# State-space input matrices built with (position, channel) on the partitions from factor rows in DRAM, and the kernel's own data moved to GpSimd's DMA queue

## The chip, the cores and the metric

One Trainium2 chip, one core. The metric is the device time of the whole program in microseconds. Before the change it is 1427.78 us, the median of three runs (1423.44 to 1439.42).

## The reference, cut to what matters

Two layers of a hybrid encoder over 256 positions of width 1024. Each layer has three branches (retention, latent attention, and a state-space layer, S5), gates, an output projection and a SwiGLU feed-forward network. The change touches the S5 branch alone in what it computes. S5 has 64 groups of 16 channels; each drives 64 complex states, in two directions d:

```python
mag = jnp.exp(dt * ar)
abar_re, abar_im = mag * jnp.cos(dt * a_im), mag * jnp.sin(dt * a_im)
bb_re = coef_re[..., None] * b_re - coef_im[..., None] * b_im
bb_im = coef_re[..., None] * b_im + coef_im[..., None] * b_re
bu = einsum('bsgc,gpc->bsgp', u_g, bb)      # complex
x_t = abar * x_{t-1} + bu_t                 # scan over s, forward for d=0, backward for d=1
y = Re(C x)                                 # summed over both directions
```

## The kernel before

**What dominates.** Nearly all weights are multiplied in three passes: ScalarE casts a raw weight tile of 512 KB to a high part (`wh`, L668), VectorE takes the rest (`wl`, L669), and TensorE runs three matmuls for each 128 rows of it (L673 to L675). A weight tile is thus 24 matmuls of 256 columns. Raw tiles come through SP's DMA queue into five buffers. This is the foreground.

**S5 is a background.** `s5` is a generator. `tick` gives it credit each time the foreground has emitted a tile or two, and a step of it is emitted while there is credit. The framework then orders the instructions of each engine by its own forecast; each engine runs its list in that order. Layer 0's S5 begins with the program; layer 1's begins before the feed-forward network of layer 0 (`begin(l + 1)`), so that its tables and matrices are made beside that network.

**Blocks of eight positions.** The scan runs over 32 blocks of 8 positions. For each of 16 steps `qq` (4 groups of channels each) an input matrix WT is needed that takes 8 positions x 16 channels = 128 rows to 256 columns (2 directions x re/im x 64 states). It is the product of a power of abar (by position) with bb (by channel). `s5_wt` makes it with the states on the partitions: VectorE multiplies a table of powers (`PW`) by `BB` in three products of 512 columns (L523, L526 twice) and adds the shared one to the other two (L531, 1024 columns). TensorE then turns it in 8 transposes of 128x128 (L536) through two PSUM banks of the pool `p5`, and ScalarE copies each bank out (L538). TensorE multiplies it with the input U in 4 matmuls (L452). After every second step ScalarE copies the product out (L459), TensorE transposes it (L462), and ScalarE writes it to the states SS in 8 small copies (L467, L468). Of `p5`'s two banks one holds the product over two steps.

Layer 0 makes WT when it is used. Layer 1 makes all 16 early, writes them to DRAM (`wtd`) and reads them back when its U is there.

**Tables.** `s5_params` makes the powers `pn` and the coefficients `cf` with (direction, group) on the partitions. `s5_tables` turns them by matmuls with a permutation (L299, L304) so that the states lie on the partitions, loads b in pieces of 16 channels (`load_b`), and makes BB on VectorE (L343 to L345).

**Output side.** After the scan, `s5_out` makes for every two steps a kernel `kf` on TensorE (L584), copies it out (L598), writes it to DRAM (`kd`) and reads it back in four skewed DMAs as a matrix M (`wt<-kd`, 128 KB each), which TensorE uses in L629. There are 16 such pairs in the two layers.

**Queues.** Every DMA is issued on SP's queue by `dma` (L121): weights, and the kernel's own data in between (wtd, kd, M, the gates parked in `gd`, u, the states, x). GpSimd only fills constants.

Of the kernel before, what the change touches and what calls it, by code (L numbers as in the profile page):

```python
# [78 lines left out]
class Kern:  # L79
# [131 lines left out]
    def s5_params(self, l):  # L211
# [47 lines left out]
        cf = self.s(2 * SP_, "t_cfn").rearrange("p (r q) -> p r q", r=2)  # L259
# [17 lines left out]
    def load_b(self, l, *bs):  # L277

        f = lambda t, k, d: self.dma(t[d * 64:d * 64 + 64].rearrange("p (g c) -> p g c", c=GC),
                                     self.a[k][l, d].rearrange("g p c -> p g c"))  # L280
        return [lambda t=t, k=k, d=d: f(t, k, d) for t, k in zip(bs, ("s5_b_re", "s5_b_im")) for d in range(2)]

    def load(self):
        if self.loads:
            f = self.loads.pop(0)
            if f:
                f()

    def s5_tables(self, l):


        nc, V, A = self.nc, self.nc.vector, self.nc.scalar
        pn, cf = yield from self.s5_params(l)
        yield 4.0
        PX = self.s4().rearrange("p (j d g) -> p j d g", j=8, d=2)
        for b in range(2):
            ps = self.bank(self.p5)
            for j in range(4):
                nc.tensor.matmul(ps[:, j * P:(j + 1) * P], pn[:, b * 4 + j].rearrange("p r q -> p (r q)"),  # L299
                                 self.perm, start=True, stop=True)  # L300
            A.copy(PX[:, b * 4:b * 4 + 4].rearrange("p j d g -> p (j d g)"), ps)
        CF = self.s(2 * 64, "t_cf").rearrange("p (r g) -> p r g", r=2)
        ps = self.bank(self.p5)
        nc.tensor.matmul(ps[:, 0:P], cf.rearrange("p r q -> p (r q)"), self.perm, start=True, stop=True)  # L304
        for r in range(2):
            for d in range(2):
                A.copy(CF[d * 64:d * 64 + 64, r, :], ps[r * 64:r * 64 + 64, d * 64:d * 64 + 64])
        PW = self.s4().rearrange("p (r s g) -> p r s g", r=2, s=8)
        A8 = self.s(2 * 64, "t_a8").rearrange("p (r g) -> p r g", r=2)
        A8s = self.s(2 * 64, "t_a8s").rearrange("p (r g) -> p r g", r=2)  # L310
        for r in range(2):
            nc.gpsimd.memset(PW[0:64, r, 0, :], 1.0 - r)
            nc.gpsimd.memset(PW[64:128, r, 7, :], 1.0 - r)
            rows = slice(r * 64, r * 64 + 64)
            A.copy(PW[0:64, r, 1:8, :], PX[rows, 0:7, 0, :])
            A.copy(PW[64:128, r, 6::-1, :], PX[rows, 0:7, 1, :])
        for d in range(2):
            rows = slice(d * 64, d * 64 + 64)
            A.copy(A8[rows, 0, :], PX[0:64, 7, d, :])
            A.copy(A8[rows, 1, :], PX[0:64, 7, d, :])  # L320
            A.mul(A8s[rows, 0, :], PX[64:128, 7, d, :], -1.0)
            A.copy(A8s[rows, 1, :], PX[64:128, 7, d, :])
        PXD = self.t(self.dr, [P, 1024], "pxd", 2)
        self.dma(PXD, PX.rearrange("p j d g -> p (j d g)"))
        if l == 0 and self.nl >= 0:
            while "b" not in self.cx:
                yield None
            br, bi = self.cx.pop("b")
        else:
            br, bi = self.s4(), self.s4()  # L330
            for f in self.load_b(l, br, bi):
                f()
        BB = [self.s4(), self.s4()]
        for qh in range(2):
            c = slice(qh * 512, qh * 512 + 512)
            nat = lambda t: t[:, c].rearrange("p (h q c) -> p h q c", h=4, q=8)
            natt = lambda t: t.rearrange("p (h q c) -> p h q c", h=4, q=8)
            cfv = lambda r: (CF[:, r, qh * 32:qh * 32 + 32].rearrange("p (q h) -> p h q", h=4)
                             .unsqueeze(3).to_broadcast([P, 4, 8, GC]))
            for r, (x, y, op) in enumerate(((br, bi, ALU.subtract), (bi, br, ALU.add))):  # L340
                yield 1.9
                t1, t2 = self.s(512, "tm"), self.s(512, "tm")
                V.tensor_tensor(natt(t1), cfv(0), nat(x), ALU.mult)  # L343
                V.tensor_tensor(natt(t2), cfv(1), nat(y), ALU.mult)
                V.tensor_tensor(BB[r][:, c].rearrange("p (q h c) -> p h q c", q=8, h=4), natt(t1), natt(t2), op)  # L345
        BBD = self.t(self.dr, [P, 2048], "bbd", 2)
        for r in range(2):
            self.dma(BBD[:, r * 1024:(r + 1) * 1024], BB[r])
        PD = self.s(512, "t_pd").rearrange("p (s g) -> p s g", s=8)
        V.tensor_tensor(PD, PW[:, 1], PW[:, 0], ALU.subtract)  # L350
        V.scalar_tensor_tensor(PW[:, 1], PW[:, 1], -1.0, PW[:, 0], ALU.mult, ALU.subtract)
        BS = self.s4()
        V.tensor_tensor(BS, BB[0], BB[1], ALU.add)
        return dict(PW=[PW[:, 0], PW[:, 1], PD], PXD=PXD, A8=A8, A8s=A8s, BB=[BS, BB[1], BB[0]], BBD=BBD)

    def s5_out_tables(self, l, tb, qh):
# [3 lines left out]
        BB2 = self.s(2 * 528, "t_bb2", 1).rearrange("p (d x) -> p d x", d=2)  # L360
        for d in range(2):
            for r in range(2):
# [834 lines left out]
    def layer(self, l, x2, acc, xg, last):  # L1197
# [44 lines left out]
        while self.loads:  # L1242
            self.load()
# [256 lines left out]
```

## Time and profile before

| | |
|---|---|
| median of three runs | 1427.78 us |
| the profiled execution | 1425.45 us, of it 1423.5 us span |
| granted TensorE clock, mean share | 0.982 |
| instructions | 27613 |
| DMA | 260.84 MB, mean 183 GB/s |
| layer 0: input matrices, about | 60 to 207 us of the span |
| layer 0: output side with M, about | 295 to 445 us |
| layer 1: input matrices, about | 549 to 803 us |
| layer 1: output side with M, about | 963 to 1130 us |

The profiled execution is 2.3 us under the median, so sums made against it stand for the median to within the spread of the runs. A busy time is a union of an engine's instructions; "idle before, releaser" is time in which an engine waited before an instruction, and what ended the wait. Matmuls overlap: a mean duration of 285 ns stands beside a start-to-start distance of about 117 ns.

### The profile page before, as it was taken

How to read it: one execution, taken by the hardware profiler on the slowest of the kernel's cores; microseconds unless marked ns; L12 is line 12 of the kernel's file. 1: busy time of each engine (PE TensorE's matmuls, PEld its weight loads, DVE VectorE, ACT ScalarE, POOL GpSimd, SP SyncE). 2: the span in 40 equal slices, each digit the busy share in tenths (PEclk: the TensorE clock that was granted, in tenths of full speed). 3: DMA queues.
4: the chain of work that ended last, by engine and by line, in shares of the span. 5: the costliest groups of instructions: out<-in, count | busy, mean ns of one | idle time of the engine just before them, and what ended most of it. 6: DMA issues, size and time to landing. Idle time of an engine off the chain costs nothing.

```text
span 1423.5 us, 27613 instructions
## 1 busy us (share of the span) xinstructions
PE 1334.4 (94%) x11102; PEld 1234.2 (87%) x11102; DVE 1042.3 (73%) x1910; ACT 807.0 (57%) x1339; POOL 4.5 (0%) x33
## 2 busy tenths in 40 slices
PE   7899998888999999999999999788999999999997
PEld 5866878867888999999999868778988899999997
DVE  7977867877687679988668547877768657777754
ACT  3656576974654455545446677786564344544442
POOL 0000000000000000000000000000000000000000
PEclk9999999999999999999999999999999999999999
DMA  8944233646786699766679784365687667666662
GB/s 218 250 146 118 69 104 99 182 137 152 211 219 194 201 211 260 210 199 197 188 229 273 239 267 131 99 193 156 157 247 188 193 200 204 181 185 187 179 179 79
DMA packets 433891, 260.84 MB, mean 183 GB/s; under 512 B 61714, under 2 KB 413284, under 8 KB 433764
## 3 DMA queue, kind: packets, MB, share of 16 engines
q1 hardware_dynamic: 433764, 259.09, 64.3%
q8 instruction: 87, 1.43, 0.4%
q14 instruction: 40, 0.33, 0.1%
HBM read 231.53 MB, written 27.53 MB: 182 GB/s over the span
## 4 chain that ended last, share of the span: by engine, by line
PE 68%; ACT 13%; DMA 8%; DVE 6%; issue 3%; SPq 1%; DVEq 0%; ACTq 0%
PE pw L673 17%; PE pw L674 17%; PE pw L675 17%; DMA wt<-kd 3%; ACT wh L668 3%; PE pw L713 2%; PE pw L714 2%; PE pw L715 2%; DVE wl L669 2%; DMA kd<-ev 2%; ACT s L497 2%; PE p L536 2%; PE p L452 2%; DMA raw<-in_w_in 1%; SPq L121 1%
## 5 line engine op out<-in xcount | busy, mean ns | idle before, releaser
L673 PE MATMUL pw<-s,wh 128*128 128x256 f32 x2472 | 714.6, 290 | 16.6 <-ACT wh L668 13.8
L675 PE MATMUL pw<-s,wl 128*128 128x256 f32 x2472 | 703.5, 285 | 8.4 <-DVE wl L669 8.3
L674 PE MATMUL pw<-s,wh 128*128 128x256 f32 x2472 | 703.0, 285 | 0.2 <-DVE s L749 0.2
L668 ACT CAST wh<-raw 128x1024 fp32r<-128x1024 f32 (+4 forms) x394 | 381.0, 972 | 456.2 <-PE pw L674 290.7
L669 DVE TENSOR_TENSOR wl<-raw,wh 128x1024 fp32r<-128x1024 f32 (+4 forms) x394 | 443.1, 1128 | 206.8 <-ACT wh L668 205.4
L673 PEld LDWEIGHTS pw<-s,wh 128*128 128x128 f32 x2472 | 472.1, 191 | 34.1 <-ACT wh L668 16.6
L675 PEld LDWEIGHTS pw<-s,wl 128*128 128x128 f32 x2472 | 472.5, 191 | 15.5 <-DVE wl L669 11.2
L674 PEld LDWEIGHTS pw<-s,wh 128*128 128x128 f32 x2472 | 472.9, 191 | 6.6 <-issue 4.8
L713 PE MATMUL pw<-s,wh 128*128 128x256 f32 x256 | 71.9, 281 | 0.0
L714 PE MATMUL pw<-s,wh 128*128 128x256 f32 x256 | 71.9, 281 | 0.0
L715 PE MATMUL pw<-s,wl 128*128 128x256 f32 x256 | 71.9, 281 | 0.0
L569 DVE TENSOR_TENSOR wy<-s,s 128x512 f32<-128x512 f32 x64 | 42.3, 687 | 16.1 <-PE pa L629 10.3
L715 PEld LDWEIGHTS pw<-s,wl 128*128 128x128 f32 x256 | 48.2, 188 | 0.0
L714 PEld LDWEIGHTS pw<-s,wh 128*128 128x128 f32 x256 | 48.2, 188 | 0.0
L713 PEld LDWEIGHTS pw<-s,wh 128*128 128x128 f32 x256 | 48.2, 188 | 0.0
L536 PE MATMUL p<-ident,wy 128*128 128x128 f32 x256 | 36.7, 276 | 11.5 <-ACT s L468 11.1
L497 ACT COPY s<-s 64x256 f32<-64x256 f32 (+1 forms) x64 | 40.7, 636 | 5.2 <-DVE s L483 4.3
L536 PEld LDWEIGHTS p<-ident,wy 128*128 128x128 f32 x256 | 28.6, 140 | 16.6 <-ACT s L468 13.2
L570 DVE TENSOR_TENSOR tm<-s,s 128x512 f32<-128x512 f32 x64 | 43.0, 687 | 0.0
L571 DVE TENSOR_TENSOR wy<-wy,tm 128x512 f32<-128x512 f32 x64 | 42.7, 685 | 0.0
L748 ACT ACTIVATE s<-ev 128x512 fp32r<-128x512 f32 x46 | 29.1, 633 | 19.7 <-DVE ev L1350 12.1
L531 DVE TENSOR_TENSOR wy<-wy,tm 128x1024 f32<-128x1024 f32 x32 | 39.1, 1221 | 0.3
(284 smaller groups left out, 1549.7 us busy)
## 6 DMA issues: line engine op xcount, KB each, us to landing
raw<-in_w_in SPq DMA_DIRECT2D x122, 512.0 KB
raw<-in_ffn_w_gu SPq DMA_DIRECT2D x88, 512.0 KB
raw<-in_w_branch SPq DMA_DIRECT2D x48, 512.0 KB
raw<-in_s_w_glu SPq DMA_DIRECT2D x32, 512.0 KB
raw<-in_ffn_w_down SPq DMA_DIRECT2D x32, 512.0 KB
wt<-kd SPq DMA_DIRECT2D x64, 128.0 KB
raw<-in_w_out SPq DMA_DIRECT2D x16, 512.0 KB
wtd<-wt SPq DMA_DIRECT2D x16, 512.0 KB
```

The source lines that it names most:

```text
L497: A.copy(*todo.pop(0))
L536: T.transpose(ps[:, i * P:(i + 1) * P], W[i % 2][:, gp * 2 + i // 2].rearrange("p s c -> p (s c)"), self.ident)
L570: V.tensor_tensor(t2, tv(1), cv(C2), ALU.mult)
L571: V.tensor_tensor(y[:, :, js, :], y[:, :, js, :], t2, ALU.add)
L668: self.nc.scalar.copy(hi, src)
L669: self.nc.vector.tensor_tensor(lo, src, hi.bitcast(F32), ALU.subtract)
L673: T.matmul(ps, lh, rh, start=first, stop=False)
L674: T.matmul(ps, lh, rl, start=False, stop=False)
L675: T.matmul(ps, ll, rh, start=False, stop=last)
L713: T.matmul(o, wh[:, k, c], xh, start=(half == 0 and m == 0 and k == 0), stop=(k == 3), **f)
L714: T.matmul(o, wh[:, k, c], xl, start=False, stop=(k == 3), **f)
L715: T.matmul(o, wl[:, k, c], xh, start=False, stop=(k == 3), **f)
```

## The change

WT is now made with (position, channel) on the partitions, so that nothing has to be turned. `s5_tables` keeps the powers and BB with (direction, group) on the partitions and writes them to DRAM as rows (`PWD`: 8 positions, `BBD`: 16 channels), in 16 DMAs of 8 partitions for PWD and 32 for BBD in each layer. For a step, `s5_fetch` reads two tiles of 512 KB: PWD's 8 rows, each repeated over 16 partitions, and BBD's 16 rows, repeated 8 times over. `s5_wt` asks for its own step's tiles and for the next step's, multiplies (L531, L532, 1024 columns each) and makes the real and the imaginary part by a subtraction and an addition of 512 columns each (L537, L538). The 8 transposes, the 2 PSUM copies and the Gauss form of the product go. BB for the output side is turned once for a layer by 16 transposes and kept in DRAM (`BB2D`). b comes in two DMAs of whole rows.

A second helper, `park`, issues a DMA on GpSimd's queue. All of the kernel's own data goes through it: 342 DMAs. SP is left with the weights, the inputs and the output. Code for loading b later (`load_b`, `load`, `nl`), which this configuration did not use, is gone.

```diff
+    def park(self, out, src):
+        return self.nc.gpsimd.dma_start(out, src)
...
     def s5_tables(self, l):
+        br, bi = self.s4(), self.s4()
+        for t, k in ((br, "s5_b_re"), (bi, "s5_b_im")):
+            self.dma(t, self.a[k][l].rearrange("d g p c -> (d g) (p c)"), pin=l > 0)
         pn, cf = yield from self.s5_params(l)
+        PN = self.s4().rearrange("p (s x) -> p s x", s=8)
...
+        A.copy(PN[0:64, 1:8, :], flat[0:64, 0:7, :])
+        A.copy(PN[64:128, 6::-1, :], flat[64:128, 0:7, :])
+        def rows(t, r0, src):
+            t = t[:, :]
+            for i in range(16):
+                at = r0 * 16384 + i // 4 % 2 * 8192 + i // 8 * 512 + i % 4 * 128
+                self.park(bass.AP(tensor=t.tensor, offset=t.offset + at, ap=[[1024, 8], [16384, 8], [1, 128]]),
+                         src[i * 8:i * 8 + 8])
+        PWD = self.t(self.dr, [8, 16384], "pwd", 2)
+        rows(PWD, 0, PN)
...
+            rows(BBD, hf * 8, B.rearrange("p c r q -> p c (r q)"))
...
+                T.transpose(ps[:, i * P:(i + 1) * P], BB[c // 8][:, c % 8].rearrange("p r q -> p (r q)"), self.ident)
...
+    def s5_fetch(self, tb, qq):
+        if qq > 15 or qq in tb["ld"]:
+            return
+        ld = tb["ld"][qq] = []
+        for k, ap in (("PWD", [[16384, 8], [0, 16], [1, 1024]]), ("BBD", [[0, 8], [16384, 16], [1, 1024]])):
+            t = self.s4()
+            src = tb[k][:, :]
+            self.park(t, bass.AP(tensor=src.tensor, offset=src.offset + qq * 1024, ap=ap))
+            ld.append(t.rearrange("p (x r q) -> p x r q", x=8, r=2))
     def s5_wt(self, tb, qq):
-        wt_ = self.s(1152, "wy")
-        k1 = self.s(512, "tm")
-        V.tensor_tensor(k1.rearrange("p (g s c) -> p g s c", g=4, s=8), pwv(0), bbv(0), ALU.mult)
-        for r in range(2):
-            w = wt_[:, r * 512:(r + 1) * 512].rearrange("p (g s c) -> p g s c", g=4, s=8)
-            V.tensor_tensor(w, pwv(1 + r), bbv(1 + r), ALU.mult)
-        V.tensor_tensor(w, w, k1.rearrange("p (o x) -> p o x", o=1).to_broadcast([P, 2, 512]), ALU.add)
-        for gp in range(2):
-            ps = self.bank(self.p5)
-            for i in range(4):
-                T.transpose(ps[:, i * P:(i + 1) * P],
-                            W[i % 2][:, gp * 2 + i // 2].rearrange("p s c -> p (s c)"), self.ident)
-            A.copy(wt[:, gp * 512:(gp + 1) * 512], ps)
+        for q in (qq, qq + 1):
+            self.s5_fetch(tb, q)
+        pw, bb = tb["ld"].pop(qq)
+        by = lambda r: pw[:, :, r:r + 1, :].to_broadcast([P, 8, 2, SP_])
+        k1, k2 = (self.s(1152, "wy")[:, 0:1024].rearrange("p (x r q) -> p x r q", x=8, r=2) for _ in range(2))
+        V.tensor_tensor(k1, bb, by(0), ALU.mult)
+        V.tensor_tensor(k2, bb[:, :, ::-1, :], by(1), ALU.mult)
+        wt = self.s(1024, "wt")
+        w = wt.rearrange("p (x r q) -> p x r q", x=8, r=2)
+        V.tensor_tensor(w[:, :, 0, :], k1[:, :, 0, :], k2[:, :, 0, :], ALU.subtract)
+        V.tensor_tensor(w[:, :, 1, :], k1[:, :, 1, :], k2[:, :, 1, :], ALU.add)
...
-            self.dma(kd, kf)
+            self.park(kd, kf)
...
-                self.dma(M[:, g4].rearrange("p q m -> p (q m)"), src)
+                self.park(M[:, g4].rearrange("p q m -> p (q m)"), src)
```

TensorE, layer 0, the first step of the input matrices. Before (`p_140`, `p_141` are the two PSUM banks of the transposes, `wt_701` the matrix, `wl_759` a weight tile's rest):

```order
L673 MATMUL pw_725<-s_34_212,wh_758 128x256
L536 MATMUL p_140_702<-ident,wy_695 128x128 x4
L536 MATMUL p_141_708<-ident,wy_695 128x128 x4
L674 MATMUL pw_725<-s_36_214,wh_758 128x256
L675 MATMUL pw_725<-s_34_212,wl_759 128x256
L452 MATMUL p_142_714<-wt_701,s_124_625 32x256 x4
L673 MATMUL pw_725<-s_34_212,wh_758 128x256
```

The same place of the changed kernel, where `wt_779` is the first matrix:

```order
L674 MATMUL pw_974<-s_38_218,wh_977 128x256
L675 MATMUL pw_974<-s_36_216,wl_978 128x256
L451 MATMUL p_148_782<-wt_779,s_128_697 32x256 x4
L673 MATMUL pw_974<-s_36_216,wh_977 128x256
L674 MATMUL pw_974<-s_38_218,wh_977 128x256
```

The eight transposes are gone, and the first product has moved back from the sixth weight tile of this phase (`wh_758`) to the ninth (`wh_977`).

VectorE, layer 0, just ahead of the first matrix of the changed kernel (`wy_775`, `wy_776` are the two products, `s_141` and `s_142` the tiles fetched from PWD and BBD):

```order
L669 TENSOR_TENSOR wl_1008<-raw_1005,wh_1007 128x1024
L669 TENSOR_TENSOR wl_1063<-raw_1060,wh_1062 128x1024
L844 TENSOR_TENSOR s_120_650<-pw_651,s_64_360 128x512
L531 TENSOR_TENSOR wy_775<-s_142_769,s_141_767 128x1024
L532 TENSOR_TENSOR wy_776<-s_142_769,s_141_767 128x1024
L846 TENSOR_TENSOR s_120_650<-s_120_650,ev_787 128x512
L537 TENSOR_TENSOR wt_779<-wy_775,wy_776 128x8x64
L538 TENSOR_TENSOR wt_779<-wy_775,wy_776 128x8x64
```

`wl_1063` is the eleventh weight rest. Before, the first two matrices stood behind the sixth. Four matrices of the changed kernel follow here before the twelfth.

GpSimd, layer 0, its list from the tables to the first fetch of the changed kernel (`pwd`, `bbd`, `bb2d` are the DRAM tables, `dud` holds the input scaled by d):

```order
L128 DMA pwd_311<-s_54_304 8x8x128 x16
L128 DMA pxd_413<-s_72_390 128x1024
L128 DMA dud_364<-s_68_365 128x1024
L128 DMA bbd_415<-s_79_416 8x8x128 x16
L128 DMA bbd_415<-s_87_459 8x8x128 x16
L128 DMA dud_364<-s_80_421 128x1024
L128 DMA bb2d_530<-s_98_531 128x1024
L128 DMA bb2d_530<-s_99_532 128x1024
L128 DMA s_141_767<-pwd_311 128x1x1024
L128 DMA s_142_769<-bbd_415 128x1x1024
```

These 55 DMAs stand one behind the other; before, GpSimd issued none, and BB went out in two DMAs on SP's queue.

## Rows read from the trace of the kernel before

**Rows 1.** The page, busy time and share of the span by engine.
```profile
PE 1334.4 (94%) x11102; PEld 1234.2 (87%) x11102; DVE 1042.3 (73%) x1910; ACT 807.0 (57%) x1339; POOL 4.5 (0%) x33
```

**Rows 2.** Windows: length, busy PE, PEld, DVE, ACT, POOL, clock, DMA share, GB/s.
```profile
455.00:490.00 35.00, 35.00 (x298) 35.00 (x298) 27.17 (x67) 18.64 (x22) 0.00 (x0) 1.00 0.62 187
735.00:805.00 70.00, 69.71 (x528) 66.39 (x528) 54.61 (x85) 41.25 (x65) 0.17 (x1) 1.00 0.83 248
```

**Rows 3.** Groups by form, PE, 62:235 (layer 0's input matrices): busy, mean | idle before.
```profile
L536 PE MATMUL p<-ident,wy 128*128 128x128 f32 x128 | 19.9, 279 | 11.2 <-ACT s L468 11.1
```

**Rows 4.** Groups by form, PE, 548:806 (layer 1's input matrices).
```profile
L536 PE MATMUL p<-ident,wy 128*128 128x128 f32 x128 | 16.8, 273 | 0.2 <-ACT wt L538 0.2
```

**Rows 5.** Timeline of PE, 119:131: start, duration, instruction [idle before <-releaser].
```profile
122.09 0.66 PE L536 MATMUL p<-ident,wy 128*128 128x128 f32 x4 [1.67 <-ACT s L468]
...
128.07 0.60 PE L536 MATMUL p<-ident,wy 128*128 128x128 f32 x4
128.51 1.03 PE L937 MATMUL pa<-s,s 128*128 128x256 f32 x4
129.40 0.66 PE L536 MATMUL p<-ident,wy 128*128 128x128 f32 x4
129.99 0.62 PE L452 MATMUL p<-wt,s 128*32 128x256 f32 x4
```

**Rows 6.** Groups by form, whole span, what the matrices cost VectorE and ScalarE.
```profile
L531 DVE TENSOR_TENSOR wy<-wy,tm 128x1024 f32<-128x1024 f32 x32 | 39.1, 1221 | 0.3
L538 ACT COPY wt<-p 128x512 f32<-128x512 f32 x64 | 35.8, 587 | 3.4 <-PE p L536 3.0
...
L523 DVE TENSOR_TENSOR tm<-s,s 128x512 f32<-128x512 f32 x32 | 21.7, 684 | 0.1
```

**Rows 7.** Timeline of DVE, 24:82: the last powers, then the sixth, ninth and tenth `wl`.
```profile
27.93 0.42 DVE L258 TENSOR_TENSOR s<-tm,tm 128x256 f32<-128x256 f32 x1
...
58.25 1.22 DVE L669 TENSOR_TENSOR wl<-raw,wh 128x1024 fp32r<-128x1024 f32 x1
...
75.97 2.35 DVE L669 TENSOR_TENSOR wl<-raw,wh 128x1024 fp32r<-128x1024 f32 x2
```

**Rows 8.** Timeline of SP's queue, 305:345: issue start, time that SP spent issuing.
```profile
311.37 0.34 SPq L121 DMA_DIRECT2D kd<-ev  x1
312.92 0.37 SPq L121 DMA_DIRECT2D raw<-in_w_branch  x1
313.39 2.53 SPq L121 DMA_DIRECT2D wt<-kd  x4
```

**Rows 9.** Chain that ended last, pieces in order of time: start, duration, what.
```profile
48.81 9.07 DMA raw<-in_w_in
...
311.37 2.00 DMA kd<-ev
315.35 5.68 DMA wt<-kd
...
553.57 0.88 PE p L536 x8
...
1117.42 2.53 DMA kd<-ev
1121.90 4.67 DMA wt<-kd
```

**Rows 10.** Groups by form, whole span: the matmuls that use M.
```profile
L629 PE MATMUL pa<-wt,s 128*32 128x128 f32 x256 | 24.3, 275 | 11.4 <-DMA wt<-kd 11.3
```

**Rows 11.** The page, all DMA packets and SP's queue.
```profile
DMA packets 433891, 260.84 MB, mean 183 GB/s; under 512 B 61714, under 2 KB 413284, under 8 KB 433764
...
q1 hardware_dynamic: 433764, 259.09, 64.3%
```

**Rows 12.** Timeline of SP's queue, 30:60, two of the loads of b.
```profile
37.48 5.54 SPq L121 DMA_DIRECT2D s<-in_s_b_im  x2
```

**Rows 13.** Timeline of PE, 48:54.
```profile
52.38 0.39 PE L673 MATMUL pw<-s,wh 128*128 128x256 f32 x1 [1.50 <-ACT wh L668]
```

More of the change, by code (lines that the diff above doesn't have):

```diff
@@ L317, in s5_tables @@
-        for d in range(2):
[L318 to L322, printed above, removed]
-        PXD = self.t(self.dr, [P, 1024], "pxd", 2)
[L324 to L339, printed above, removed]
+        for d in range(2):
+            rows_ = slice(d * 64, d * 64 + 64)
+            A.copy(A8[rows_, 0, :], PX[0:64, 7, d, :])
+            A.copy(A8[rows_, 1, :], PX[0:64, 7, d, :])
+            A.mul(A8s[rows_, 0, :], PX[64:128, 7, d, :], -1.0)
+            A.copy(A8s[rows_, 1, :], PX[64:128, 7, d, :])
@@ L340, in s5_tables @@
+        PXD = self.t(self.dr, [P, 1024], "pxd", 2)
+        self.park(PXD, PX.rearrange("p j d g -> p (j d g)"))
+        BBD = self.t(self.dr, [16, 16384], "bbd", 2)
+        nat = lambda t, hf: t.rearrange("p (q c) -> p c q", c=GC)[:, hf * 8:hf * 8 + 8, :]
+        cfv = lambda r: cf[:, r:r + 1, :].to_broadcast([P, 8, SP_])
+        BB = []
+        for hf in range(2):
+            B = self.s4().rearrange("p (c r q) -> p c r q", c=8, r=2)
             for r, (x, y, op) in enumerate(((br, bi, ALU.subtract), (bi, br, ALU.add))):
@@ L341, in s5_tables @@
                 yield 1.9
[L342 to L354, printed above, removed]
+                t1, t2 = (self.s(512, "tm").rearrange("p (c q) -> p c q", c=8) for _ in range(2))
+                V.tensor_tensor(t1, cfv(0), nat(x, hf), ALU.mult)
@@ L356, in s5_out_tables @@
+        for qh in range(2):
+            self.park(BB2D[:, qh * 1024:(qh + 1) * 1024], half[qh].rearrange("p d q h c -> p (d q h c)"))
+        return dict(ld={}, PWD=PWD, BBD=BBD, BB2D=BB2D, PXD=PXD, A8=A8, A8s=A8s)
     def s5_out_tables(self, l, tb, qh):
@@ L726, in fm_pair_native @@
             self.flush()
-            self.load()
             self.tick(3.5)
@@ L1202, in layer @@
         native = lambda c: self.fm_pair_native(a["w_in"][l], OFF_U + c * 256, xk(xg))
-        if l == 0 and self.nl >= 0:
-            bs = [self.s4(), self.s4()]
-            self.loads = [None] * self.nl + self.load_b(0, *bs) + [lambda: self.cx.update(b=bs)]
-            self.loads += [lambda k=k: self.table(k) for k in ("rope", "rel")]
         self.pin = self.pinm > 1
@@ L1239, in layer @@
             dus.append(du)
-            if not (l == 0 and self.nl >= 0):
-                self.dma(dud[:, qh * 1024:(qh + 1) * 1024], du)
-        while self.loads:
-            self.load()
-        if l == 0 and self.nl >= 0:
-            for qh in range(2):
-                self.dma(dud[:, qh * 1024:(qh + 1) * 1024], dus[qh])
+            self.park(dud[:, qh * 1024:(qh + 1) * 1024], du)
         del du, dus
```

98 lines of the change are left out of this document (43 added, 55 removed).

## The prediction

> **What bounds the kernel now.** I read the page first: TensorE is busy 94% of the span, VectorE 73%, ScalarE 57%, GpSimd nothing [rows 1]. A busy share of pipelined matmuls could hide slack, so the windows come next. In the feed-forward stretch 455 to 490 TensorE runs 298 matmuls in 35 us, 0.117 us each, at the full granted clock (1.00 of 2.4 GHz) with no gap, so a weight tile of 24 matmuls takes 2.8 us; the DMA engines are at 0.62 [rows 2]. Where layer 1's last input matrices and the start of its foreground meet (735 to 805), TensorE is still full and the DMA share is 0.83. So TensorE's own work is the limit, and what is taken from it is gained unless something arrives later in its place. The groups then show what the transposes of the input matrices cost it [rows 3, 4], the chain shows the round trip of M through DRAM just in time on the path [rows 9, 10], and the timeline of SP's queue shows what issuing those DMAs takes [rows 8].
>
> **What goes from TensorE.** 32 steps lose 8 transposes each, 64 groups of four. In layer 0 a group lasts, from its start to the next instruction's, 0.44 us (128.07 to 128.51) to 0.59 us (129.40 to 129.99) [rows 5]; I take 0.52, so 32 groups are 16.6 us. In layer 1 a set of eight stands in the chain with 0.88 us [rows 9], and 16 of them are 14.1 us. Ahead of the transposes TensorE also sat idle for 11.2 us in layer 0 and 0.2 us in layer 1, nearly all of it until ScalarE's small copies to the states (L468) had freed a bank of `p5` [rows 3, 4] (one such wait, of 1.67 us, stands in [rows 5]). Both banks are then used by the product and its transpose alone. The change adds 16 transposes in each layer for the output side, 8 groups, 4.2 us. The sum is 30.7 + 11.4 - 4.2 = 38 us. What is late next is the product itself (L451), which waits for VectorE's last operation on the matrix; I let 4 us of the idle time come back there, and count **-34 us**.
>
> **ScalarE and VectorE.** ScalarE loses 64 copies of 0.587 us, 36 us [rows 6], off the path: nothing counted. VectorE paid 3 x 0.684 + 1.221 = 3.27 us for a step and pays 2 x 1.221 + 2 x 0.684 = 3.81 us [rows 6], 0.54 us more, 17 us over 32 steps. It is idle for a quarter of the span and for 8 of 35 us even beside the feed-forward network [rows 1, 2], so I count nothing; without that cover it is 17 us.
>
> **The start of layer 0.** Here the change puts a new wait in front of both engines. VectorE's first product stands behind the eleventh weight rest instead of the sixth, and it waits for the first fetch, which stands behind 53 others on GpSimd's list (16 for PWD, 32 for BBD, five whole tables), itself with its twin making 55. Behind the waiting product VectorE holds the twelfth weight rest, and TensorE the ninth tile. The last powers are made at 28.3 us [rows 7]; with ScalarE's copies GpSimd starts at about 30 us. If a DMA holds its queue for g us, the first matrix is ready at 30 + 55 g, plus some 3 us for the landing and 3.8 us for the products: 37 + 55 g. TensorE comes to the first product in its ninth tile. The sixth rest is made at 58.3 us [rows 7]; TensorE is about two tiles behind it and has three to go, so 58 + 5 x 2.8 = 72, and I take 73 us. No row shows g. From below, SP's shortest own issue is 0.34 us [rows 8]: ready at 56 us, no stall. From above, one DMA at a time at kd's 2.0 us from issue to landing [rows 9]: ready at 147 us, a stall of 74 us. The nearest row is SP's 2.53 us for four skewed reads, 0.63 each [rows 8]; I take a third more, 0.85, for a queue that no row shows. That is ready at 84 us, a stall of **+11 us** (0 to +74).
>
> **The round trip of M.** 16 pairs. From the issue of kd to the landing of M it took 9.7 us in the first of nine pairs of the chain and 9.2 us in the last (311.37 to 321.03, 1117.42 to 1126.57; nine pairs, 9.0 to 11.1) [rows 9]. TensorE waits 11.4 us for M in all [rows 10], 0.7 us a pair: M comes just in time, so what lengthens the trip shows. On GpSimd's queue, kd's issue may take 0.4 us more, and four skewed reads at 1.2 us (twice SP's 0.63, as each has 256 pieces) take 4.8 us instead of 2.5. Against that, M's last read landed 5.7 us after its issue while a weight tile had been issued 0.5 us ahead of the four, and kd, with nothing ahead of it, landed in 2.0 [rows 8, 9]; in a queue without weights I take 2.0 us off. Net 0.7 us a pair, **+11 us**. Bounds: -11 (all of the wait goes) to 16 x (4 x 2.0 - 2.5 + 1.6) = +114 us.
>
> In the Trainium skill, DMA: Bandwidth & Descriptors, Anatomy of one DMA, a DMA of GpSimd's queue costs 2.0 us and its bytes at 436 GB/s, so kd 2.6 us and a read of M 2.3 us, which run one behind the other in flight. By that the trip would be no longer than the rows show, and this term would be near 0. No row of this trace has such a DMA.
>
> **DMA traffic.** 64 fetches of 0.52 MB add 33.6 MB to 259 MB, which took 64.3% of the engines [rows 11]: 8 points more on the whole. In a stretch it is tighter. The new order has six steps over the last 15 weight tiles of layer 1's matrices, 42 us at 2.8 us a tile: 6 x 1.05 MB / 42 us = 150 GB/s on top of 248 GB/s at a share of 0.83 [rows 2], where a share of 1 would be 299 GB/s. If nothing gives, that stretch needs 56 us instead of 42. The fetches run a step ahead and can lag by one, so I take **+6 us** (0 to +14).
>
> **What SP's queue gains.** b came in pieces of 64 B (61714 packets under 512 B on the page, rows 11), and two of its four loads held SP for 5.54 us [rows 12]; a weight tile issued behind them at 48.81 us took 9.07 us to land [rows 9], and TensorE then waited 1.50 us for its cast [rows 13]. b is now two loads of whole rows, and SP no longer waits for the kernel's own data. I count **-5 us** (-9 to 0).
>
> **The sum.** -34 + 11 + 11 + 6 - 5 = -11 us against the profiled execution's 1425.45 us: **1414 us**. That execution is 2.3 us below the median, which is inside the spread of the runs. A measurement of this kernel tells about 1%, 14 us, from no change.
>
> **Rivals.**
>
> *GpSimd's queue is slow, and the kernel slower than before.* GpSimd has never issued a DMA in this trace, 342 of them are now in one list in order, and both places above wait on its pace. With g = 1.2 us at the start and 1.8 us for a skewed read, the start stalls for 37 + 66 - 73 = 30 us, and M's trip grows by 7.2 - 2.5 + 0.7 - 2.0 = 3.4 us, 54 us in 16 pairs: -34 + 30 + 54 + 6 - 5 = +51, **1476 us**. It decides from where the two waits together exceed 33 us: at my g for M from g = 1.05 at the start, or at my g for the start from 1.55 us for a read of M. For it: M is just in time [rows 10]. Against it: the 0.63 us of SP's issue [rows 8].
>
> The Trainium skill, SBUF — State Buffer, Two separate sides (the trap "DVE blocks DMA"), speaks for this rival: GpSimd cannot write the descriptors of its DMAs while VectorE runs a copy-like operation in a two-port mode. Most of VectorE's time here is two-input `TENSOR_TENSOR`, which that page says has no such mode. No run here shows it.
>
> *The DMA engines become the bound.* The fetches of layer 1 collide with weights, and VectorE waits for a fetch with weight rests behind it. If the 14 us of the tight stretch come in full, and again beside the feed-forward network, where 16 steps spread over some 90 tiles, at about half that (7 us), the sum is -34 + 11 + 11 + 21 - 5 = +4, **1429 us**. For it: 0.83 at 735 to 805 [rows 2]. Against it: M's reads already repeat rows of a small table and land in 5 us.
>
> The Trainium skill, DMA: Bandwidth & Descriptors, Rules for kernel authors (use all 16 engines), speaks for it: a DMA whose outermost dimension counts 8 runs on at most 8 of the 16 engines, and both fetches are of that kind. No run here shows what such a fetch takes.
>
> *Everything new is hidden.* g stays at SP's 0.63 us, the start does not stall (37 + 35 = 72), and M comes sooner: -38 - 5 + 3 = -40, **1386 us**. For it: TensorE is all that is full [rows 2].
>
> **How the numbers follow.** Forecast 0.50, with 1398 to 1432 as its own range; slow queue 0.25; DMA-bound 0.10; all hidden 0.15. Faster by over 1% (under 1413.5 us by the median): half of the forecast's range and all of the last, 0.26 + 0.15 = 0.41. Slower by over 1% (over 1442): 0.23 of the slow queue, 0.05 of the forecast, 0.01 of the DMA-bound case, 0.29. Within 1%: 0.30. The range leaves out one in ten on either side: below, most of the hidden case is kept (1384), above, the slow queue up to its price of 1476.
>
> **What would show it.** Right: no L536 group, 28 us less of TensorE's matmul time, L451 with only small waits. VectorE's wait at its first L531 shows the start (11 us forecast) and gives g by GpSimd's spacing. The wait ahead of L629 shows M (11 us before, 22 forecast). The DMA share from 735 to 805 shows the traffic. The forecast is wrong if the first two waits together exceed 45 us or vanish, or if VectorE waits for fetches all through both layers.

## The result, and the profile after

The changed kernel takes 1588.84 us (median of 4 runs, 1577.31 to 1593.49) against 1428.37 us (4 runs), a ratio of 1.110 with an interval of 1.101 to 1.119. That is 160 us slower where 14 us faster were forecast, and far above the range. The profiled execution is at 1591.1 us with a span of 1589.3 us, 165.8 us longer than before.

The page of the changed kernel, the rows that answer to [rows 1, 11], with the granted clock and the DMA share in 40 slices:

```profile
PE 1374.7 (86%) x10874; PEld 1262.4 (79%) x10874; DVE 1059.8 (67%) x1904; ACT 779.6 (49%) x1293; POOL 223.0 (14%) x375
...
PEclk9977999789998999979999899999999899999999
DMA  7999985444855578899999996455557556666662
...
DMA packets 398564, 297.67 MB, mean 187 GB/s; under 512 B 34578, under 2 KB 367716, under 8 KB 398436
...
q1 hardware_dynamic: 359172, 201.67, 49.5%
q0 software_dynamic: 39264, 94.25, 22.9%
```

TensorE runs 228 matmuls fewer (11102 to 10874) and is busy 40 us longer: the mean granted clock falls from 0.982 to 0.930. q0 is GpSimd's queue. The two queues together moved 14% more bytes and took 72.4% of the engines instead of 64.3%, yet from about 40 to 240 us and from about 600 to 950 us the DMA digits stand at 8 or 9.

To see where the time went I align both kernels by the foreground: the n-th low half `wl` (L669) is the same weight tile in both. This table is worked out from the starts of those instructions (VectorE's timeline), us:

```
n-th wl            11    12    20    65   109   141    219    257    309    389
before           80.0  88.2 126.0 286.1 480.3 580.8  821.8  950.7 1162.3 1389.8
after - before   -1.9  25.7  35.2  41.5  83.3  82.2  122.4  124.4  165.8  165.9
e2 - before       3.2   2.4   0.1   2.5  34.2  38.4   37.3   44.2   76.4   76.4
e4 - before      -3.0   2.6   3.4  -0.5  41.8  39.4   31.6   36.1   71.4   71.7
e7 - before      -3.1  13.8   1.1   2.1  44.0  41.0   36.8   36.6   70.8   70.8
e18 - before     -2.0   0.7   0.1  -3.1   5.9   2.1   -9.1   -8.5    1.4    1.5
```

(e2, e4, e7 and e18 are experiments below.) The loss comes in four stretches of about 41 us: layer 0's input matrices (to the 65th tile), layer 0's output side with the round trip of M (to the 109th), layer 1's input matrices (141 to 219) and layer 1's output side (257 to 309). Elsewhere at most 2 us are lost.

Those four as windows. Columns: from:to, length, busy PE, PEld, DVE, ACT, POOL, granted clock, DMA share, GB/s. First the kernel before, then the changed one:

```profile
0.00:286.10 286.10, 251.64 (x1681) 213.33 (x1682) 223.41 (x567) 183.15 (x343) 2.18 (x17) 0.96 0.55 148
286.10:480.30 194.20, 179.87 (x1768) 158.56 (x1767) 146.40 (x267) 110.17 (x195) 1.52 (x10) 0.98 0.66 184
...
580.80:821.80 241.00, 240.71 (x1930) 233.87 (x1929) 179.01 (x237) 124.89 (x171) 0.65 (x4) 1.00 0.74 219
...
950.70:1162.30 211.60, 200.03 (x1969) 184.03 (x1968) 145.91 (x206) 118.61 (x214) 0.16 (x2) 0.98 0.67 189
```

```profile
0.00:327.60 327.60, 240.54 (x1541) 209.03 (x1542) 222.73 (x536) 163.20 (x309) 56.25 (x111) 0.89 0.82 184
327.60:563.60 236.00, 203.69 (x1806) 175.50 (x1805) 153.46 (x294) 114.97 (x206) 45.64 (x67) 0.91 0.58 158
...
662.90:944.20 281.30, 246.58 (x1788) 235.38 (x1787) 195.54 (x252) 108.36 (x136) 27.46 (x47) 0.93 1.00 246
...
1075.10:1328.20 253.10, 219.43 (x1979) 196.98 (x1978) 152.30 (x230) 125.37 (x225) 44.35 (x59) 0.92 0.61 163
```

Where the matrices are made the DMA share goes from 0.55 to 0.82 and from 0.74 to 1.00. On the output side it falls, so the DMA engines are not the cause there. TensorE's wait for M has quadrupled and its matmuls are slower: the group that answers to [rows 10], a line of GpSimd's reads of M, and VectorE's first operation on a matrix:

```profile
L629 PE MATMUL pa<-wt,s 128*32 128x128 f32 x256 | 42.5, 352 | 46.2 <-DMA wt<-kd 46.0
...
L128 POOL DMA_DIRECT2D wt<-kd x64 | 59.0, 926 | 53.5 <-DMA kd<-ev 31.1
L531 DVE TENSOR_TENSOR wy<-s,s 128x1024 f32<-128x1024 f32 x32 | 39.1, 1222 | 36.9 <-DMA s<-bbd 36.9
```

46.2 us of waiting where it was 11.4, and a mean of 352 ns where it was 275. The wait is paid twice here: the granted clock of layer 0's output stretch fell from 0.98 to 0.91; by the clock's records TensorE was at the lower level (1.2 GHz) for 44 us of it, where it was 7 us before. The stretch is 42 us longer, but only 18 us of that is idle time (32.3 instead of 14.3 us, length less busy PE); most of the rest is the same work at the lower clock (TensorE was busy for 39 us at the lower level instead of 6, and about half of such time is what that level adds, an estimate; there are 38 matmuls more).

At the start, GpSimd's timeline (issue start, time spent issuing) and then VectorE's, with the first products:

```profile
63.34 3.87 POOL L128 DMA_DIRECT2D bbd<-s  x7 [0.28 <-issue]
67.20 0.59 POOL L128 DMA_DIRECT2D dud<-s  x1
67.78 1.10 POOL L128 DMA_DIRECT2D bb2d<-s  x2
68.87 0.62 POOL L128 DMA_DIRECT2D s<-pwd  x1
69.47 0.63 POOL L128 DMA_DIRECT2D s<-bbd  x1
```

```profile
86.69 1.23 DVE L531 TENSOR_TENSOR wy<-s,s 128x1024 f32<-128x1024 f32 x1 [6.75 <-DMA s<-bbd]
...
96.68 1.22 DVE L531 TENSOR_TENSOR wy<-s,s 128x1024 f32<-128x1024 f32 x1 [5.82 <-DMA s<-bbd]
```

GpSimd issues a DMA about every 0.56 us, faster than the 0.85 I took. But the first pair of fetches, issued at 68.87 and 69.47, has landed only at 86.7, 17 us after the second issue. Pieces of the chain that ended last show how long transfers took when several fetches were in flight (start, duration, what):

```profile
71.77 31.91 DMA s<-bbd
...
664.18 38.90 DMA raw<-in_ffn_w_gu
```

One fetch took 32 us, and a weight tile that came between fetches 39 us.

### The profile page after: what moved, and what is told of

The parts are those of the page before. It is cut to its first block, busy times and chain, and to the rows that moved or that the text cites. A ratio compares the mean times of both kernels' runs of the same rounds, so it can differ in the third digit from the quotient of the medians.

```text
span 1589.3 us, 27444 instructions
## 1 busy us (share of the span) xinstructions
PE 1374.7 (86%) x10874; PEld 1262.4 (79%) x10874; DVE 1059.8 (67%) x1904; ACT 779.6 (49%) x1293; POOL 223.0 (14%) x375
## 4 chain that ended last, share of the span: by engine, by line
PE 43%; DMA 23%; issue 14%; DVE 8%; ACT 7%; POOL 5%; DVEq 0%; SPq 0%; POOLq 0%; ACTq 0%
PE pw L675 11%; PE pw L673 11%; PE pw L674 11%; DMA wt<-kd 4%; DMA raw<-in_w_in 4%; DMA s<-bbd 4%; DMA kd<-ev 2%; DMA raw<-in_ffn_w_gu 2%; DVE wl L669 2%; POOL wt L128 2%; DMA s<-in_rel 2%; ACT s L497 2%; ACT wh L668 1%; PE pa L629 1%; POOL bbd L128 1%
## 5 line engine op out<-in xcount | busy, mean ns | idle before, releaser
L673 PE MATMUL pw<-s,wh 128*128 128x256 f32 x2472 | 728.5, 295 | 32.0 <-ACT wh L668 25.3
L674 PE MATMUL pw<-s,wh 128*128 128x256 f32 x2472 | 715.8, 290 | 1.5 <-DVE s L745 0.8
L668 ACT CAST wh<-raw 128x1024 fp32r<-128x1024 f32 (+3 forms) x394 | 381.5, 971 | 558.9 <-PE pw L674 309.6
L669 DVE TENSOR_TENSOR wl<-raw,wh 128x1024 fp32r<-128x1024 f32 (+3 forms) x394 | 443.1, 1128 | 228.1 <-ACT wh L668 227.7
L673 PEld LDWEIGHTS pw<-s,wh 128*128 128x128 f32 x2472 | 486.7, 197 | 51.5 <-ACT wh L668 28.5
L674 PEld LDWEIGHTS pw<-s,wh 128*128 128x128 f32 x2472 | 487.5, 197 | 6.9 <-issue 3.4
L629 PE MATMUL pa<-wt,s 128*32 128x128 f32 x256 | 42.5, 352 | 46.2 <-DMA wt<-kd 46.0
L713 PE MATMUL pw<-s,wh 128*128 128x256 f32 x256 | 72.7, 285 | 1.6 <-ACT s L744 1.2
L714 PE MATMUL pw<-s,wh 128*128 128x256 f32 x256 | 72.4, 283 | 0.0
L629 PEld LDWEIGHTS pa<-wt,s 128*32 128x32 f32 x256 | 19.4, 136 | 60.5 <-DMA wt<-kd 58.6
L128 POOL DMA_DIRECT2D wt<-kd x64 | 59.0, 926 | 53.5 <-DMA kd<-ev 31.1
L531 DVE TENSOR_TENSOR wy<-s,s 128x1024 f32<-128x1024 f32 x32 | 39.1, 1222 | 36.9 <-DMA s<-bbd 36.9
L713 PEld LDWEIGHTS pw<-s,wh 128*128 128x128 f32 x256 | 48.5, 190 | 3.0 <-ACT s L744 1.4
L714 PEld LDWEIGHTS pw<-s,wh 128*128 128x128 f32 x256 | 48.5, 190 | 0.1
L673 PE MATMUL pw<-wh,s 128*128 128x512 f32 (+1 forms) x96 | 37.0, 394 | 13.1 <-DVE s L844 5.4
L451 PE MATMUL p<-wt,s 128*32 128x256 f32 x256 | 22.0, 421 | 27.4 <-DVE wt L538 27.2
```

Of the source, the lines that this page charges most:

```text
L128: return self.nc.gpsimd.dma_start(out, src)
L629: T.matmul(po[g4 * 32:g4 * 32 + 32, oc:oc + 128], lhsT, rhs, start=(k == 0), stop=(k == 2), tile_position=(0, g4 * 32))
L668: self.nc.scalar.copy(hi, src)
L669: self.nc.vector.tensor_tensor(lo, src, hi.bitcast(F32), ALU.subtract)
L673: T.matmul(ps, lh, rh, start=first, stop=False)
L674: T.matmul(ps, lh, rl, start=False, stop=False)
```

## The experiments

Theory A, formed from these rows: two separate causes. The fetches fill the DMA engines far beyond their bytes and delay the weights (about 85 us). GpSimd's queue lengthens the round trip of M (about 82 us). Rival B: the queue alone. Rival C: the fetches alone, M being late because of them. Times without an interval are one execution, beside one of the kernel before on the same chip: 1423.27 us for e1 to e8, 1434.17 us for e13 to e16; by several, its median was 1427.42 us for e9 to e12 and 1428.44 us for e17 and e18. The kernel before spread over 15 us in 13 executions (1421.65 to 1436.63 us), so a difference of that size between single executions shows nothing.

### The queue and the traffic apart: e2, e4, e1, e3, e8

**e2**, the kernel before with `park` in place of `dma` for its own data:

```
-            self.dma(kd, kf)
+            self.park(kd, kf)
...
```

> The kernel before with its own data (not the weights and inputs) in GpSimd's queue and nothing else changed. Theory A: the M stretches lose about 80 us, the rest nothing, 1495 to 1520 us. Theory B: as A or more, 1500 to 1590 us, with weights late where the matrices of layer 1 are written out. Theory C: no loss, 1420 to 1440 us.

Measured: 1501.86 us, 79 us more. By the table above the loss stands in the two output stretches (32 us each, with 4 and 7 us in between), as theory A says; C falls.

**e4**, the changed kernel with one pair of fetches a layer:

```
+        if qq:
+            tb["ld"][qq] = tb["ld0"]
+            return
-        ld = tb["ld"][qq] = []
+        ld = tb["ld"][qq] = tb["ld0"] = []
```

> The changed kernel with the two fetches of step 0 alone in each layer; all 16 steps use them, so 60 of the 64 fetches and their 31 MB are left out, and the matrices of steps 1 to 15 are made from the rows of step 0. Theory A: the stretches of input matrices come back and give the transposes' gain as well, 1475 to 1505 us, the M stretches stay late. Theory B: little, 1550 to 1590 us. Theory C: M comes in time too, 1390 to 1430 us.

Measured: 1496.97 us, 92 us less than the changed kernel. Both matrix stretches come back and the output side stays late. B falls.

**e1**, `park` issues on SP (the edit below), and **e3**, only kd and M back on SP:

```
-        return self.nc.gpsimd.dma_start(out, src)
+        return self.nc.sync.dma_start(out, src)
```

> The changed kernel with all 342 own DMAs back in SP's queue. Theory A (two causes: the fetches fill the DMA engines and delay the weights, about 85 us in the two stretches of input matrices; GpSimd's queue lengthens the round trip of M, about 82 us in the two stretches of the output side): the M stretches come back, the others stay, 1490 to 1525 us, TensorE's wait ahead of L629 near 11 us. Theory B (the queue alone: in a second queue the 4 KB packets overtake the weights; in one queue they do not): about 1390 to 1430 us. Theory C (the fetches alone, M being late because they are): no gain, 1560 us or more, and worse where a fetch that waits for its buffer holds up the weights behind it.

> The changed kernel with the write of kd and the four reads of M alone back in SP's queue (80 of the 342 DMAs). Theory A: 1500 to 1520 us, the stretches of input matrices unchanged. Theory B (all of the queue): a part, 1500 to 1550 us. Theory C: 1575 to 1600 us.

Measured: e1 1581.52 us, e3 1543.19 us. In e1 the wait for M is cured (20.0 us of weight loads waiting for it instead of 58.6), but the matrix stretches get worse: they lose 52 and 61 us against the kernel before, instead of 42 and 40, and VectorE waits 96.2 us for fetches instead of 36.9. The number is the one that C gave, but C has fallen by e2; what fits is the clause in its text: a fetch that waits for its buffer, and the tables' 48 small writes, hold up the weights behind them in one queue. Theory A had left that out. What of it is the writes is read from e5 and e18 below. e3 gives back 46 us, less than the 80 that I gave to M alone.

**e8**, as e2 but with kd and M left on SP:

```
-            self.park(kd, kf)
+            self.dma(kd, kf)
...
```

> The kernel before with its own data in GpSimd's queue, except the write of kd and the four reads of M, which stay in SP's. If the round trip of M is all that GpSimd's queue costs: 1420 to 1435 us. If its other transfers cost too, or disturb M (gate values, output tables): 1445 to 1490 us.

Measured: 1451.43 us. So in the order of before, M's 80 DMAs cost 50 us on GpSimd (1501.86 - 1451.43) and the other own data 28 us. The trip itself, worked out from the starts of the issues and of the matmuls (mean of 16 pairs, us):

```
                 kd issue to    the four    last M issue to   kd issue to
                 first M issue  M issues    last M matmul     last M matmul
before (SP)          3.03         2.58          6.56             11.59
after (GpSimd)       4.11         3.69          8.14             15.02
e2 (GpSimd)          3.65         3.69          8.27             14.68
e3 (SP)              3.09         2.60          7.91             12.95
e11 (two and two)    2.81         2.38          8.81             13.09
e18 (SP)             2.85         2.52          7.02             11.79
```

A pair takes 3.4 us longer on GpSimd: 1.1 us before the reads can be issued, 1.1 us for issuing them (0.92 us each) and 1.6 us from the last issue to the last use. (The columns add up to more than the whole, since the last issue, 0.92 us on GpSimd and 0.6 on SP, is in two of them.) Where the first 1.1 us go is read from kd's packets in the DMA records (means of 16): the first starts 1.8 us after the start of the issue instead of 1.1, they take 1.3 us in all instead of 1.4, and M's first read is issued 1.0 us after the last of them instead of 0.5. So the bytes of kd move no more slowly; the time goes before and behind them.

**e11**, the kernel before with two of M's four reads on GpSimd:

```
-                self.dma(M[:, g4].rearrange("p q m -> p (q m)"), src)
+                (self.nc.gpsimd.dma_start if g4 % 2 else self.dma)(M[:, g4].rearrange("p q m -> p (q m)"), src)
```

> The kernel before with two of M's four reads issued by GpSimd and two by SP at the same time. If M's trip is held by the four issues one behind the other (2.5 us): 1410 to 1420 us. If it is held by the landing: no change, 1420 to 1432 us. If a read in GpSimd's queue is slow to land or to signal: 1445 to 1490 us.

Measured: 1455.49 us (4 runs), ratio 1.019, 1.013 to 1.025, so 28 us slower. Issuing from two queues saves little: by the row of the trip the issues are 0.2 us shorter, and from the last issue to the last use it takes 2.3 us longer. GpSimd's reads of M landed here in 6.2 us (median of 32), while the last reads of M in SP's queue that stand in the chain of the kernel before took 3.4 to 5.7 us. So a read in GpSimd's queue lands late also when few are queued. Why it does was not found.

### What makes a fetch slow: e6, e7, e9, e13 to e17

A fetch is 512 KB, the size of a weight tile, so bytes alone do not explain it. **e6**, **e16**, **e7** and **e17** keep the bytes and give each partition 4 KB of its own from the table of the input vectors. All four read the whole of that table, 1 MB, in each step; only the form of the source differs:

```
-            (changed)  [[16384, 8], [0, 16], [1, 1024]]  and  [[0, 8], [16384, 16], [1, 1024]]
+            e6         [[32768, 8], [1024, 16], [1, 1024]]
+            e16        [[16384, 16], [1024, 8], [1, 1024]]
+            e7         [[1024, 128], [1, 1024]]
+            e17        [[2048, 128], [1, 1024]]
```

> The changed kernel with fetches of the same 512 KB, still with an outermost dimension of 8, but each of the 128 partitions reads 4 KB of its own from the table of the input vectors instead of sharing 8 or 16 rows (the matrices are made from wrong rows, nothing is left out). If it is the repeated rows that make a fetch slow: landing of the first fetches under 10 us and 1510 to 1540 us. If it is the bytes, or the 8: 1575 to 1600 us.

> The same with an outermost dimension of 128 (again 4 KB of its own for each partition, wrong rows, nothing left out). If the outermost count of 8 holds a fetch to half of the DMA engines: a fetch alone lands in about 4.5 us instead of 6.4, 1510 to 1550 us. If it is the bytes: as the kernel with 8, 1575 to 1600 us.

> The changed kernel with fetches of 16 rows, each of eight adjacent pieces of 4 KB, a piece of its own for every partition and rows 64 KB apart, outermost dimension 16 (the matrices are made from wrong rows, nothing is left out). If the outermost count decides: as with 128, 1490 to 1515 us. If the 64 KB pitch does: as with 8, 1560 to 1590 us.

> The changed kernel with fetches of 128 rows of 4 KB, one for each partition, 8 KB apart in DRAM, outermost dimension 128 (the matrices are made from wrong rows, nothing is left out). If the outermost count decides: as the 128 rows in one piece, 1490 to 1505 us, landing near 8 us. If that run was fast because its 512 KB lay in one piece: 1540 to 1590 us.

Measured: e6 1576.52, e16 1544.51, e7 1496.02, e17 1509.61 us. With 128 rows outermost all 64 fetches cost no more than leaving 60 of them out (e4, 1496.97). Own rows instead of repeated ones (e6) change little, and taking the 512 KB apart (e17) gives 14 us more, which is within the spread. The DMA issues of the changed kernel, of e16 and of e7 (KB each, median us to landing):

```profile
s<-pwd POOLq DMA_DIRECT2D x32, 512.0 KB, 13.6
s<-bbd POOLq DMA_DIRECT2D x32, 512.0 KB, 15.3
```

```profile
s<-bbd POOLq DMA_DIRECT2D x64, 512.0 KB, 10.8
```

```profile
s<-bbd POOLq DMA_DIRECT2D x64, 512.0 KB, 8.2
```

The stretch of layer 1's matrices in e7, against 281.30 us at a share of 1.00 and 246 GB/s:

```profile
621.80:858.60 236.80, 230.14 (x1787) 222.47 (x1787) 195.08 (x252) 108.17 (x136) 25.80 (x50) 0.99 0.95 291
```

More bytes a second at a lower share. And the packets of the stretch 70 to 100 us, worked out from the DMA records (GpSimd's packets of 4 KB, mean duration, their rate, and the mean of the weights' packets of 2 KB in the other queue):

```
             outermost   4 KB packets   GB/s   weights' 2 KB packets
after             8         289 ns      135          156 ns
e6                8         284 ns      146          142 ns
e16              16         223 ns      215          127 ns
e7              128         165 ns      325           87 ns
e17             128         163 ns      315           89 ns
```

**e13** and **e15** leave the outermost 8 and move the rows (68 KB apart instead of 64; side by side):

```
-            PWD = self.t(self.dr, [8, 16384], "pwd", 2)
+  e13       PWD = self.t(self.dr, [8, 17408], "pwd", 2)
-  (source)  [[16384, 8], [0, 16], [1, 1024]]
+  e15       [[1024, 8], [0, 16], [1, 1024]]
```

> The changed kernel with the two tables' rows 68 KB apart in DRAM instead of 64 KB, fetches as they are (outermost 8), nothing left out. If the 64 KB pitch makes the rows collide in DRAM: the fetches land twice as soon and 1495 to 1530 us. If the outermost count of 8 holds them: unchanged, 1575 to 1600 us.

> The changed kernel with each step's rows side by side in the tables (8 rows in 32 KB, 16 rows in 64 KB), fetches with an outermost dimension of 8, nothing left out. If the spread of the addresses is what makes a fetch slow: 1495 to 1535 us. If it is the outermost count of 8: unchanged, 1575 to 1600 us.

Measured: 1587.99 and 1577.77 us. The place of the rows in DRAM is not it.

**e9** tries the remedy: the powers' table with every row twice, fetched with 16 outermost rows, the input vectors in eight DMAs of 64 KB (16 rows each); **e14** is the same with a pitch of 68 KB.

```
+            if k == "PWD":
+                self.park(t, at([[16384, 16], [0, 8], [1, 1024]]))
+            else:
+                for s in range(8):
+                    self.park(t[s * 16:s * 16 + 16], at([[16384, 16], [1, 1024]]))
```

> The changed kernel with the same rows in the same places, but each fetch cut so that its outermost dimension is 16: the powers' table has every row twice (16 more small writes, in SP's queue) and is fetched by one DMA, the input vectors by eight DMAs of 64 KB, one for each position, seven more issues a step on GpSimd. If the outermost count decides, as the run with 128 says: 1500 to 1525 us, the stretches of input matrices as there. If that run was fast for another reason (rows of its own, long contiguous reads): 1570 to 1620 us, worse by GpSimd's 224 more issues.

> The kernel with fetches cut to an outermost dimension of 16, and the rows 68 KB apart, nothing left out. If count and pitch both matter: 4 KB packets near 160 ns, 1495 to 1535 us. If pitch does not matter and the cut did not help for another reason: as without the pitch, 1560 to 1585 us.

Measured: 1573.69 and 1578.86 us, no remedy. Their packets stay slow (252 ns in e9 from 70 to 100 us), and GpSimd waits for its own earlier fetches (56.3 and 24.5 us in this row) before it issues the next:

```profile
L128 POOL DMA_DIRECT2D s<-bbd x256 | 123.4, 489 | 165.5 <-DMA s<-pwd 56.3 <-DVE gnb L962 26.0 <-DMA s<-bbd 24.5
```

So the form of the fetch decides: 128 outermost rows, one for each partition, are fast; 16 help by less than half of that; 8 are slow wherever they lie. The kept traces say a little more, worked out from the DMA records. A fetch that had no other fetch beside it never had more than 10 of its 4 KB packets in flight at once when 8 rows were outermost (changed kernel, e6, e13, e15), and up to 18 with 16 or 128 rows (e16, e7, e17). In the changed kernel such a fetch landed in 6.4 us (issued at 609.1), in e7 in 4.2 us (572.0). So the outermost count limits how wide one fetch runs. But from 70 to 100 us several fetches were in flight and the DMA engines were full in both kernels (share 1.04 at 224 GB/s in the changed kernel, 1.03 at 401 in e7); there it is the time of a packet that differs, and e16, as wide as e7, still has 223 ns against 165. An 8-row fetch also carries 128 packets of 4 bytes that a fetch of 16 or 128 rows does not have; at their mean of 12 ns, 64 such fetches make about 6 us on 16 engines (an estimate from these counts), so their own time does not explain it.

Why the packets are slower, and why 16 is not enough, stays open: no row tells which DMA engine a packet ran on. A fetch of repeated rows cannot have 128 outermost rows without a table sixteen and eight times as large, which was not tried.

### Both causes away: e12, e10, e5, e18

**e12** leaves table rows and fetches on GpSimd and puts all else back on SP (fetches as in the change); **e10** is e12 with e9's fetches. **e5** is e4 with everything on SP; **e18** is e4 with the table rows and its four fetches on GpSimd and all else on SP:

```
-            self.park(kd, kf)
+            self.dma(kd, kf)
...
```

> The changed kernel with the table rows and the fetches alone in GpSimd's queue and all other own data back in SP's, fetches as they are (outermost 8). Theory A in two sums: the M stretches fall to what the run with everything in SP's queue had, the input matrices stay: 1505 to 1525 us. If what was left after M alone went back (1543 us) is not the queue: 1540 us.

> Both remedies together: fetches with an outermost dimension of 16, table rows and fetches alone in GpSimd's queue, all else in SP's, nothing left out. Theory A, if the two causes add: 1425 to 1450 us, which is what is left when the transposes' gain is given back to M's shorter cover and the later scan. If the gain of the transposes shows after all: under 1415 us.

> The changed kernel with the fetches of step 0 alone (as in the run before, 31 MB left out) and all own data back in SP's queue: what the change leaves when both suspects are away. Theory A, with the transposes' 34 us a true gain: 1385 to 1405 us. Theory A, with that gain lost to the new order of the work (later first product, less cover ahead of M): 1415 to 1445 us. If a third cost is still there: above 1450 us.

> The changed kernel with the fetches of step 0 alone (60 of 64 fetches left out, wrong matrices), the table rows and these fetches in GpSimd's queue and all other own data in SP's: both suspects away, and SP no longer held by the tables' small writes. If SP's queue made most of the 31 us that the run with all in SP's queue was above the kernel before: 1420 to 1435 us. If the new order costs them: 1445 to 1460 us. If the transposes' gain of 34 us shows in full: under 1405 us.

Measured: e12 1528.35; e10 1517.80 (4 runs, ratio 1.062, 1.057 to 1.068), far from the 1425 to 1450 I expected, since e9's fetches do not help; e5 1454.09; e18 1425.85 (10 runs, ratio 0.998, 0.995 to 1.001). So the 28 us between e5 and e18 are the tables' small writes and the four fetches in SP's queue ahead of the weights. And with the two causes away the time is that of before: 1588.84 - 1496.97 = 92 us for the fetches, 1496.97 - 1425.85 = 71 us for GpSimd's queue. In the other order, by e12, the queue is 60 us and the fetches 102, so the two overlap by some 11 us. Both e4 and e18 leave 31 MB of fetches out; a run with all 64 fetches in e7's form and the queues of e18 was not made.

e18 also shows what the transposes were worth once nothing stands in the way: nothing that can be measured, or at most 0.5% by the interval. Its windows of the four stretches:

```profile
0.00:283.00 283.00, 235.96 (x1577) 206.89 (x1578) 226.43 (x555) 168.55 (x319) 30.02 (x67) 0.93 0.57 158
283.00:486.20 203.20, 189.02 (x1791) 165.77 (x1790) 149.37 (x276) 109.59 (x197) 1.37 (x10) 0.96 0.64 182
...
582.90:812.70 229.80, 225.86 (x1766) 219.05 (x1765) 191.55 (x251) 107.80 (x134) 0.16 (x1) 0.99 0.79 233
...
942.20:1163.80 221.60, 204.02 (x1979) 187.35 (x1980) 151.41 (x230) 125.17 (x225) 0.16 (x2) 0.98 0.65 182
```

Layer 1's matrices gain 11.2 us (241.0 to 229.8), near the 14.1 forecast. In layer 0 TensorE's busy time falls by 15.7 us and its idle time rises by 12.6 (34.5 to 47.0), so 3.1 us are left. Then the two output stretches are 9.0 and 10.0 us longer, though the trip of M is that of before: the new order puts its pairs later among the weight tiles (the last kd is issued after the 297th `wl`, not the 294th). That this order is the reason was not isolated.

## Why the prediction was wrong

**The start.** The formula's first part was near: GpSimd starts at 30.15 us and issues at 0.56 us, which gives 30 + 55 x 0.56 = 61 us; with some 9 us of waits in between, on other engines and on its own transfers, the first fetch was issued at 68.9, still before the 77 us that 0.85 gives. The step that failed is "plus some 3 us for the landing". It took 17 us, as eight fetches were issued within 9 us. Part of that is their number alone: in e7, with 128 rows outermost, the second fetch took 11.4 us. 11 us were forecast for the stall; the lag is 35 us by the 20th tile, and 1 us in e7.

**DMA traffic, +6 us (0 to +14).** The largest miss. I priced the fetches by their bytes, at the 299 GB/s that a full share would give: 33.6 MB as if they ran like weights. At a share of 1.00 layer 1's stretch moved 246 GB/s. The range did not allow for a fetch that runs at half the rate and beside which the weights' packets take 156 ns, where they take 87 ns beside fetches with 128 rows. Together with the start it is 92 us (e4). The rival "The DMA engines become the bound" named the mechanism and had a tenth of the chance; its price went by bytes too.

The Trainium skill, DMA: Bandwidth & Descriptors, Rules for kernel authors (use all 16 engines), which I named and did not price, says that an outermost dimension of 8 confines a DMA to at most 8 engines. The traces agree for a fetch alone: at most 10 of its packets were in flight at once, against up to 18, which fits half as many engines. The page asks for a multiple of 16, ideally the 128 partitions, and has no price for the one against the other; here 16 gave 1544.51 us and 128 gave 1496.02 and 1509.61.

**The round trip of M, +11 us (-11 to +114).** Right in place and in sign, wrong in size: the step that failed is "I take 2.0 us off" for a queue without weights. A pair grew by 3.4 us, which is the price in the slow-queue rival, though by another sum (a read is issued in 0.92 us, not 1.8, and its data is used later after the issue); that the two agree is luck. Wait and clock together cost 50 us in e2 against e8. I had also not counted that the other own data, off the path before, costs 28 us in GpSimd's queue. Of the blocking by VectorE, which that rival had on its side, nothing is seen in the issues: kd's 16 took 545 to 591 ns each, beside a VectorE that is busy 67% of the span.

The Trainium skill's price for a DMA of GpSimd's queue (DMA: Bandwidth & Descriptors, Anatomy of one DMA) would have left this term near 0. The trace does not agree: kd landed in 3.0 us and a read of M in 5.5 us (medians of the changed kernel), and the trip is longer by 3.4 us.

**TensorE, -34 us.** The transposes' work is gone and TensorE's matmul time falls, but the step "what is taken from it is gained" held only for layer 1's matrices (11 us). [Rows 2] were read there and beside the feed-forward network, where TensorE has no gap; layer 0 had 34.5 us of idle time in 286, and the output side is a chain of waits. So even with both causes away the change is worth nothing that can be measured (ratio 0.995 to 1.001).

**SP's queue, -5 us.** Not seen apart: in e18 the eleventh tile is 2.0 us earlier, the twelfth 0.7 us later.

The signs that I had named came out: the first two waits together are 53 us (6.75 at the first L531, 46.2 ahead of L629), over the 45 that I had set, and VectorE waits for fetches in both layers (22.3 and 14.6 us).

## What to carry to other kernels

Price a new transfer by its form as well as by its bytes: measure a DMA with the same access pattern, alone and several at once, before 64 of them go into stretches that are already at a share of 0.55 and 0.74. A write and read back through DRAM that is just in time belongs in the queue with the shorter trip; here 18 us more of idle time in a stretch came with 24 us more of busy time, as TensorE ran at the lower level for 44 us of it instead of 7. An idle-free window shows what an engine's work is worth in that window alone; read it in each stretch where the work is taken away.

## What the runs showed that was not expected

A GpSimd DMA costs little to issue (0.56 us, 0.92 for a read of M), and still 80 of them in place of SP's cost 50 us. A fetch of 512 KB with 8 outermost rows not only ran at less than half the rate of one with 128 (135 against 325 GB/s), it also made the packets of the other queue take 156 ns instead of 87. And the DMA share of layer 1's matrix stretch is near full in both cases, 1.00 at 246 GB/s and 0.95 at 291: a full share does not say how many bytes move.
